# Queries' and keys' parts side by side in DRAM with fewer transfers, pairs five to seven turned from their own place, five output units held behind attention's last output

## The chip, the cores and the metric

The kernel runs as one program on one core of a Trainium2 chip. The metric is the device time of one execution in microseconds. Before the change the median of three runs is 1719.52 us (1718.66 to 1720.41).

## The reference, cut to what matters

One layer of a streaming encoder for a prompt of 1024 tokens and for 8 streams of 16 new tokens each ("samples"), width 1024, in fp32:

```python
qkv = rmsnorm(x, g_mix) @ w_in            # q, k, v of group A (8 heads of 64) and of group B (8 heads of 64)
a   = stick_breaking(q_a, k_a, v_a)       # causal, sigmoid weights, no softmax
o_b = chunk_band(q_b, k_b, v_b, rel)      # softmax over own chunk of 64 and 8 before, with a bias by distance
mix = concat(rmsnorm(a), rmsnorm(o_b))    # per head
x   = x + mix @ w_out
x   = x + (silu(h @ w_gate) * (h @ w_up)) @ w_down,   h = rmsnorm(x, g_ffn)
x   = x + sigmoid(rmsnorm(x) @ w_ple_gate) * (p @ w_ple_proj)
```

The samples attend to cached keys and values of 1024 past frames (group A) or 512 (group B). The outputs are the final norm and the new keys and values.

## The kernel before, in words

The 1024 prompt tokens are 8 row tiles of 128 and the samples one more, so there are nine. Every fp32 product is made from parts: a high part (rounded) and a low part (the rest), so that one product of two matrices is three matmuls (lines 100 to 102: high x high, low x high, high x low). The program's stages follow each other on one core: the projection of x to q, k and v; attention; the output projection; the feed-forward network; the embedding.

**Queries and keys through DRAM.** The projection leaves queries and keys transposed. `parts` cuts a group of 384 tokens into high and low, side by side in one tile `sq`; `transposed_out` (line 242) stores them to DRAM with two transfers, one into the tensor of the high parts and one into that of the low parts (`qT0h`, `qT0l`, `kT0h`, ... with 0 for group A and 1 for group B; there are 48 groups). Values are stored likewise (`v`, line 283).

**Attention** (`attention`, a generator of 137 steps) works on 8 pairs of heads, 0 to 3 of group A and 4 to 7 of group B. Each pair has 16 units: two heads by eight row tiles. When a head begins, `head` (line 531) loads its queries and keys: `qk` has 128 partitions and three parts of 1024, the queries with the high part in the first 64 partitions and the low part in the other 64, the keys' high part twice, the keys' low part twice; six transfers of 256 KB. For heads of group B `bias` then loads a table `toep` (line 553), which GpSimd negates (line 555). A unit is made in a pipeline: scores S (579, 580), weights w on ScalarE, VectorE and GpSimd, five steps later the weights' transposition (610) and its parts (614 and `sub`), two steps later for every second unit the output `po` (633, 634), which ScalarE copies to `ob` (637). After a head's last unit `turn` transposes `ob` back into `osb` (648), and after a pair's second head `finish` scales `osb` (671) and, for pairs 0 to 6, stores it to DRAM as `mixp` (674).

**What runs beside attention.** Attention's steps alternate with those of other generators: first with the rest of the projection, then with group 1 of the samples' attention over the cache (`draw`, lines 141, 405, 468; its results go out as `mixs`, line 486) and the embedding's products, and its last 36 steps with `side`. `side` is the first half of the output projection, that over pairs 0 to 3. It brings a pair's rows back from DRAM in three groups of three tiles (`mixn`, lines 894 and 898, four buffers), transposes and cuts them (904, 907, 908), loads half of the weight columns (`wraw`, then `whi` and `wlo`; two pairs of buffers), and makes 18 units, two column halves by nine tiles, each of 12 matmuls into `acc` (lines 100 to 102), one addition and one store (933, 937, 938). Then it brings pairs 4 to 6. When attention has ended, the rest of `side` is run, then pair 7, whose groups are transposed from `osb` itself but for the samples' tile, and then the weights of the second half are loaded and cut. The second half (the products `ps`), the norm and the transposition of its rows (`hrow`, line 1030) follow.

**What sets the order.** Each engine runs its instructions in one fixed order, which a framework makes from the program's order and its own planning. All transfers go through one queue, that of SyncE, and are issued in order.

Of the kernel before, what the change touches and what calls it, by code (L numbers as in the profile page):

```python
# [13 lines left out]
F32 = mybir.dt.float32  # L14
# [3 lines left out]
ALU = mybir.AluOpType  # L18
# [4 lines left out]
P = 128  # L23
D = 1024
KT = 8
NP = 8
NT = 9
HD = 64
# [4 lines left out]
SKEW = 2  # L33
R2 = 1.2
LAG, RAWS, PT = 5, 7, 2
VLAG, AHEAD = (2, 1), 2


@with_exitstack
def tile_hymba_step(  # L40
# [37 lines left out]
    nc = tc.nc  # L78
# [20 lines left out]
    def mm3(out, ah, al, bh, bl, start, stop):  # L99
        T.matmul(out, lhsT=ah, rhs=bh, start=start, stop=False)  # L100
        T.matmul(out, lhsT=ah, rhs=bl, start=False, stop=False)  # L101
        T.matmul(out, lhsT=al, rhs=bh, start=False, stop=stop)  # L102
# [111 lines left out]
    mixp = [dram.tile([P, NP, P], F32, name=f"mixp{i}") for i in range(7)]  # L214
# [12 lines left out]
    def qkv(ch, hT, stg, first, second):  # L227

        def parts(n, src, scale=1.0):
            both = stg.tile([P, 2, 384], F32R, name="sq", tag="sq")  # L230
            hl = [both[:, x, :n] for x in range(2)]
            if scale == 1.0:
                A.copy(hl[0], src)
                sub(V, hl[1], src, hl[0])
            else:
                A.activation(hl[0], src, AF.Copy, scale=scale)
                V.scalar_tensor_tensor(hl[1], src, scale, hl[0].bitcast(F32), op0=ALU.mult, op1=ALU.subtract)
            return [x.bitcast(F32) for x in hl]
# [95 lines left out]
    def decode(grp, ch, dk):  # L334
# [26 lines left out]
        parts = {}  # L361
        for what in "qk":
            for x in range(2):
                t_ = dk.tile([P, 4, P], F32, name=f"s{what}{x}", tag="slo" if x else f"s{what}", bufs=1)
                nc.sync.dma_start(t_, qkT[grp]["qk".index(what)][x][:, :, NP * P :].rearrange("c p n -> p c n"))
# [144 lines left out]
            yield  # L510


    kept = []

    def attention(ap_, ps, lag):
        def prepare(p8):
# [6 lines left out]
        def head(st, hh):  # L523

            grp, pr = st["grp"], st["pr"]
            hs = slice(hh * 64, hh * 64 + 64)
            (qh, ql), (kh, kl) = [[qkT[grp][w][x][pr] for x in range(2)] for w in range(2)]
            qk = ap_.tile([P, 3 * D], F32R, name="qk", tag="qk", bufs=2)
            for j, parts in enumerate(((qh, ql), (kh, kh), (kl, kl))):
                for i in range(2):  # L530
                    nc.sync.dma_start(qk[i * 64 : i * 64 + 64, j * D : (j + 1) * D].bitcast(F32), parts[i][hs, :D])
# [86 lines left out]
        def outputs(st, hh, g, wt):  # L618
            wth, wtl = wt
            grp = st["grp"]  # L620
            base = max(0, 2 * g - 4) if grp else 0
            nkb = 2 * g + 2 - base
            po = ps["t"].tile([P, 512], F32, name="po", tag="T")
            order = [2 * g] + [kb for kb in range(base, 2 * g + 2) if kb != 2 * g]
            for i, kb in enumerate(order):
                c0, c1 = 0, 256
                if kb == 2 * g + 1:
                    c0 = P
                if grp and kb == 2 * g - 4:
# [4 lines left out]
                T.matmul(dst, lhsT=vs, rhs=wtl[:, kb - base, c0:c1], start=False, stop=(i == nkb - 1))  # L634
# [21 lines left out]
        def finish(st):  # L656

            pr, grp, osb = st["pr"], st["grp"], st["osb"]
            ss = st["ss"].rearrange("p h t -> p (h t)")
            if grp:  # L660
                rs = st["rs"].rearrange("p h t -> p (h t)")
                V.reciprocal(rs, rs)
                V.tensor_tensor(ss, ss, rs, op=ALU.mult)
                V.tensor_tensor(ss, ss, rs, op=ALU.mult)
                r = rstd_of(ap_, ss, 2 * NP, 1.0 / HD, "o")
                G.tensor_tensor(r, r, rs, op=ALU.mult)
            else:
                r = rstd_of(ap_, ss, 2 * NP, 1.0 / HD, "o")
            for hh in range(2):
                own = osb[:, :, hh * HD : (hh + 1) * HD]  # L670
                G.tensor_tensor(own, own, r[:, hh * NP : (hh + 1) * NP].unsqueeze(2).broadcast_to([P, NP, HD]),
                                op=ALU.mult)
            if grp * 4 + pr < 7:
                nc.sync.dma_start(mixp[grp * 4 + pr], osb)

        def run(p8s):
# [42 lines left out]
    ps = {}  # L719
# [139 lines left out]
    def chain(*parts):  # L859
        for p_ in parts:  # L860
            yield from p_
# [23 lines left out]
    mp = pool(dstack, "mp", "right", 2)  # L885
    banks(dstack, "right", m=2)

    def fetch_mix(k, g):

        n = min(3, NP - g * 3)  # L890
        m = mp.tile([P, 3, P], F32, name="mixn", tag="mixn", bufs=4)
        src = m[:, :n]
        if k < 7:
            nc.sync.dma_start(src, mixp[k][:, g * 3 : g * 3 + n])
        else:
            src = pairs[7]["osb"][:, g * 3 : g * 3 + n]
        if n < 3:
            nc.sync.dma_start(m[:, 2], mixs[k // 4][:, (k % 4) * P : (k % 4 + 1) * P])
        return [src[:, o] if o < n else m[:, 2] for o in range(3)]

    def turn_mix(k, g, srcs):
        pt = ps["m"].tile([P, 384], F32, name="pt", tag="M")
        for o, src in enumerate(srcs):
            T.transpose(pt[:, o * P : (o + 1) * P], src, ident)
        h, l = hT.rows(g, k)
        gk = g_out[:, k : k + 1]
        A.activation(h, pt, AF.Copy, scale=gk)
        V.scalar_tensor_tensor(l, pt, gk, h.bitcast(F32), op0=ALU.mult, op1=ALU.subtract)

    def mix(ks):  # L910

        got = []
        for k in ks:
            while k not in done:
                yield
            for g in range(3):
                got.append((k, g, fetch_mix(k, g)))
                if len(got) > 2:
                    turn_mix(*got.pop(0))
                yield  # L920
        for x in got:
            turn_mix(*x)
            yield

    def half_out():

        yield from mix(range(4))
        for c in range(2):
            wh, wl = out_weights(0, c)
            for t in range(NT):  # L930
                cs = slice(c * 512, (c + 1) * 512)
                xs = mp.tile([P, 512], F32, name="xs", tag="xs", bufs=3)
                nc.sync.dma_start(xs, x_tok[t][:, cs])
                acc = ps["m"].tile([P, 512], F32, name="acc", tag="M")
                for k in range(4):
                    mm3(acc, *hT.tok(t, k), wh[:, k], wl[:, k], k == 0, k == 3)
                V.tensor_tensor(xs, xs, acc, op=ALU.add)
                nc.sync.dma_start(resid[t * P : (t + 1) * P, cs], xs)
                yield

    def out_weights(grp, c):

        return ch.load(w_out[0, grp * 512 : grp * 512 + 512, c * 512 : (c + 1) * 512].rearrange("(k p) c -> p k c", p=P),
                       4, 512)
# [146 lines left out]
    marks = []  # L1091

    A.activation(xg.tile([P, 1], F32, name="any", tag="r_n"), nhalf[:, 0:1], AF.Sigmoid)
    order = [0, 4, 1, 5, 2, 6, 8, 3, 7]
    xs, first_half, rows = {}, {}, []
    fetch(order[0], 0)
    with ExitStack() as planned:
# [618 lines left out]
```

## Time and profile before

| | |
|---|---|
| median of 3 runs | 1719.52 us (1718.66 to 1720.41) |
| the profiled execution | 1712.64 us |
| its span, first to last instruction | 1710.6 us |
| TensorE clock granted, mean | 0.99 |
| bytes by DMA | 293.49 MB |
| attention's last output `po` begins | 793.41 us |
| first transposition of `hrow` (L1030) | 822.69 us |

The profile shows one execution on the core. Busy time of an engine is counted without register, branch, semaphore and DMA-issuing instructions. PE is TensorE's matmul, PEld its weight load, DVE VectorE, ACT ScalarE, POOL GpSimd, SP SyncE; L904 is line 904 of the kernel. A row of the timeline has start, duration, engine, line, operation, out<-in, shape and count, and in brackets the idle time of the engine before it and what ended it. A row of a stretch has its bounds, its length, each engine's busy time with its count of instructions, the mean clock granted to TensorE, the mean busy share of the 16 DMA engines, and GB/s. In the list of DMA issues the last number is the median time from issue to landing.

### The profile page before, as it was taken

The numbers are of one execution on the slowest core, as the hardware profiler recorded it, in microseconds if no ns is written. First come the engines' busy times: TensorE is split into PE (matmuls) and PEld (weight loads), VectorE is DVE, ScalarE is ACT, GpSimd is POOL, SyncE is SP. The second block draws the span as 40 slices with busy tenths as digits, with TensorE's granted clock in tenths as the row PEclk, the third lists the DMA queues.
The fourth block names the chain that finished last, engine by engine and source line by source line (L and its number), as shares of the span: only waits on it lengthen the run. The fifth ranks groups of instructions, "written<-read, shape, count | busy, mean of one in ns | idle before, by whom it ended". The sixth has DMA issues, their size and how long they took to land.

```text
span 1710.6 us, 27738 instructions
## 1 busy us (share of the span) xinstructions
PE 1651.7 (97%) x10308; PEld 1421.3 (83%) x10308; DVE 1099.0 (64%) x1716; ACT 807.1 (47%) x1713; POOL 805.7 (47%) x652
## 2 busy tenths in 40 slices
PE   8999999989997999898989999999999999999998
PEld 7999888989996887787868888888888878878887
DVE  6111444379889666854787666666565597798875
ACT  5323545366778777643543233333332244433673
POOL 2313301277356411322345555555555379968763
PEclk9999999999998999999999999999999999999999
DMA  5847888665369885854422222222222597722222
GB/s 193 276 151 219 275 292 293 187 187 168 116 181 277 276 266 163 252 176 169 153 82 96 96 96 95 96 93 87 86 89 95 214 367 256 257 79 111 99 98 99
DMA packets 172810, 293.49 MB, mean 172 GB/s; under 512 B 16642, under 2 KB 96258, under 8 KB 170371
## 3 DMA queue, kind: packets, MB, share of 16 engines
q1 hardware_dynamic: 172674, 291.71, 52.0%
q8 instruction: 82, 1.34, 0.3%
q14 instruction: 54, 0.43, 0.1%
HBM read 204.77 MB, written 86.90 MB: 171 GB/s over the span
## 4 chain that ended last, share of the span: by engine, by line
PE 78%; DVE 7%; DMA 6%; ACT 3%; POOL 3%; issue 2%; SPq 1%; POOLq 0%; DVEq 0%; ACTq 0%
PE ps L1058 24%; PE ps L100 6%; PE ps L101 6%; PE ps L102 6%; PE pt L1321 4%; PE pt L1058 3%; PE ps L1321 3%; PE pt L610 2%; PE pt L405 2%; PE acc L468 2%; DMA v<-sv 2%; DVE keep L114 2%; PE po L634 1%; PE sdec L427 1%; PE S L579 1%
## 5 line engine op out<-in xcount | busy, mean ns | idle before, releaser
L105 POOL TENSOR_TENSOR wlo<-wraw,whi 128x512 fp32r<-128x512 f32 (+1 forms) x119 | 211.3, 1798 | 139.7 <-ACT whi L159 138.5
L100 PE MATMUL ps<-whi,hTh 128*128 128x256 f32 x576 | 167.7, 291 | 1.3 <-ACT st L267 1.3
L101 PE MATMUL ps<-wlo,hTh 128*128 128x256 f32 x576 | 164.2, 285 | 0.0
L102 PE MATMUL ps<-whi,hTl 128*128 128x256 f32 x576 | 163.7, 284 | 0.1
L159 ACT CAST whi<-wraw 128x512 fp32r<-128x512 f32 (+1 forms) x122 | 88.6, 744 | 71.4 <-PE ps L1058 28.6
L100 PEld LDWEIGHTS ps<-whi,hTh 128*128 128x128 f32 x576 | 110.4, 192 | 7.9 <-issue 5.7
L592 POOL TENSOR_TENSOR w<-w,keep 128x127 f32<-128x127 f32 (+4 forms) x64 | 78.6, 1230 | 74.8 <-DVE keep L114 64.5
L102 PEld LDWEIGHTS ps<-whi,hTl 128*128 128x128 f32 x576 | 110.4, 192 | 0.8 <-DVE hTl L105 0.4
L101 PEld LDWEIGHTS ps<-wlo,hTh 128*128 128x128 f32 x576 | 110.5, 192 | 0.2
L614 ACT CAST wth<-pt 128x512 fp32r<-128x512 f32 (+1 forms) x192 | 84.4, 466 | 44.5 <-PE pt L610 43.9
L105 DVE TENSOR_TENSOR wtl<-pt,wth 128x512 fp32r<-128x512 f32 (+1 forms) x192 | 94.1, 513 | 14.8 <-ACT wth L614 14.7
L114 DVE TENSOR_TENSOR_SCAN keep<-keep,zero 128x128 f32<-128x128 f32 (+7 forms) x64 | 101.6, 1588 | 1.7
L610 PE MATMUL pt<-ident,w 128*128 128x128 f32 x528 | 90.4, 284 | 8.5 <-DVE wtl L105 4.4
L610 PEld LDWEIGHTS pt<-ident,w 128*128 128x128 f32 x528 | 64.2, 144 | 21.6 <-DVE wtl L105 6.0
L579 PE MATMUL S<-qk 128*128 128x384 f32 (+2 forms) x192 | 71.9, 376 | 6.5 <-ACT keep L583 4.4
L633 PE MATMUL po<-wth,vk 128*128 128x256 f32 (+1 forms) x304 | 76.5, 283 | 1.5 <-DVE wtl L105 1.2
L105 POOL TENSOR_TENSOR actl<-actr,acth 128x1024 fp32r<-128x1024 f32 (+1 forms) x22 | 61.2, 2782 | 34.2 <-DMA sr<-acts 20.7
L634 PE MATMUL po<-wtl,vk 128*128 128x256 f32 (+1 forms) x304 | 73.4, 285 | 0.0
L406 DVE COPY kT<-pt 128x512 f32<-128x512 f32 x48 | 33.0, 687 | 53.4 <-PE pt L405 49.5
L101 PE MATMUL ps<-hTl,whi 128*128 128x384 f32 x192 | 65.4, 341 | 0.0
L102 PE MATMUL ps<-hTh,wlo 128*128 128x384 f32 x192 | 65.3, 340 | 0.0
L100 PE MATMUL ps<-hTh,whi 128*128 128x384 f32 x192 | 65.3, 340 | 0.0
(441 smaller groups left out, 5292.1 us busy)
## 6 DMA issues: line engine op xcount, KB each, us to landing
draw<-in_cache_sb_k SPq DMA_DIRECT2D x32, 512.0 KB, 5.7
draw<-in_cache_sb_v SPq DMA_DIRECT2D x32, 512.0 KB, 5.7
act<-sg SPq DMA_DIRECT2D x11, 1152.0 KB
actr<-act SPq DMA_DIRECT2D x22, 576.0 KB, 9.5
wraw<-in_w_in SPq DMA_DIRECT2D x11, 1024.0 KB, 8.7
wraw<-in_w_gate SPq DMA_DIRECT2D x11, 1024.0 KB, 5.5
wraw<-in_w_up SPq DMA_DIRECT2D x11, 1024.0 KB, 5.4
v<-sv SPq DMA_DIRECT2D x36, 256.0 KB, 4.7
```

The costliest lines, as they stand in the source:

```text
L100: T.matmul(out, lhsT=ah, rhs=bh, start=start, stop=False)
L101: T.matmul(out, lhsT=ah, rhs=bl, start=False, stop=False)
L102: T.matmul(out, lhsT=al, rhs=bh, start=False, stop=stop)
L105: return eng.tensor_tensor(out, a, hi.bitcast(F32), op=ALU.subtract)
L114: V.tensor_tensor_scan(rev, rev, zero[:, 0:1].to_broadcast([P, n - d]), keep[:, n - d : n - d + 1], op0=ALU.mult, op1=ALU.max)
L159: A.copy(h[:, o], v[:, o])
L579: T.matmul(sc, lhsT=hd["qq"][:, qs], rhs=hd["kkh"][:, kc], start=True, stop=False)
L610: T.transpose(pt[:, (c - c0) * P : (c - c0 + 1) * P], w[:, c * P : (c + 1) * P], ident)
L614: A.copy(wth[:, ks, qs], pv)
L634: T.matmul(dst, lhsT=vs, rhs=wtl[:, kb - base, c0:c1], start=False, stop=(i == nkb - 1))
L1058: T.matmul(out, lhsT=a[x][:, k], rhs=b[y][:, k], start=(not more and k == 0 and n == 0), stop=(k == 3 and n == 2), skip_group_check=more)
L1321: T.matmul(out, lhsT=a[i][:, x, m * P : (m + 1) * P], rhs=b[j][:, x], start=(not more and x == 0 and n == 0), stop=(x == 1 and n == 2), sk ...
```

## The change

The edit does the following:

- `qkT` is one tensor for both parts, `[4, 128, 2, 1152]`, with high and low side by side. A group is stored by one transfer instead of two (96 become 48). A head is loaded by three transfers instead of six (96 become 48): one for the queries, both parts, and two for the keys, both parts, one for each half of the partitions.
- The queries' load has a source written as `r x n -> x r n`: part, row, column, that is 2 x 64 x 1024; its destination is 128 partitions x 1024.
- `mixp` has five tensors instead of seven. Pairs 5, 6 and 7 are transposed straight from `osb` (`direct`).
- The samples' rows `mixs` are loaded whole, once, into two tiles (`own`), instead of by eight small loads. `mixn` has three buffers instead of four.
- `side` becomes `first_done(half_out())`: at each step it is asked whether pair 5, then pair 6, is done; if so that pair is turned, otherwise the next step of `half_out` is taken. `half_out` brings pairs 0 to 3, makes nine units of the first column half, four of the second, and brings pair 4.
- Five units of the second column half are held: they are made after attention's generator has ended, and are not issued before the last `po`.
- The tiles' order is `[0, 4, 1, 5, 2, 6, 8, 3, 7]` instead of 0 to 8.
- The low part of the second weight tile of the second half is made by VectorE instead of GpSimd.

```diff
-    qkT = [[[dram.tile([4, P, NT * P], F32, name=f"{nm}T{g}{n}") for n in "hl"] for nm in "qk"] for g in range(2)]
+    qkT = [[dram.tile([4, P, 2, NT * P], F32, name=f"{nm}T{g}") for nm in "qk"] for g in range(2)]
...
-        def transposed_out(grp, w, c, g, hl):
-            for x in range(2):
-                nc.sync.dma_start(qkT[grp][w][x][c, :, g * 384 : (g + 1) * 384], hl[x])
+        def transposed_out(grp, w, c, g, both):
+            nc.sync.dma_start(qkT[grp][w][c, :, :, g * 384 : (g + 1) * 384], both)
...
-            for j, parts in enumerate(((qh, ql), (kh, kh), (kl, kl))):
-                for i in range(2):
-                    nc.sync.dma_start(qk[i * 64 : i * 64 + 64, j * D : (j + 1) * D].bitcast(F32), parts[i][hs, :D])
+            nc.sync.dma_start(qk[:, :D].bitcast(F32), q.rearrange("r x n -> x r n"))
+            for i in range(2):
+                nc.sync.dma_start(qk[i * 64 : i * 64 + 64, D:].rearrange("p (x n) -> p x n", x=2).bitcast(F32),
+                                  k)
...
-            if grp * 4 + pr < 7:
+            if grp * 4 + pr < 5:
                 nc.sync.dma_start(mixp[grp * 4 + pr], osb)
...
+    own = [at.tile([P, 7 * P], F32, name="mixs0", tag="keep0")[:, :512], mp.tile([P, 512], F32, name="mixs1", bufs=1)]
+    for t_, m in zip(own, mixs):
+        nc.sync.dma_start(t_, m)
...
-        m = mp.tile([P, 3, P], F32, name="mixn", tag="mixn", bufs=4)
+        m = mp.tile([P, 3, P], F32, name="mixn", tag="mixn", bufs=3)
...
+    def direct(k):
+        for g in range(3):
+            turn_mix(k, g, sources(k, g, pairs[k]["osb"][:, g * 3 : min(g * 3 + 3, NP)]))
+            yield
...
+    def first_done(rest):
+
+        for k in (5, 6):
+            while k not in done:
+                next(rest, None)
+                yield
+            yield from direct(k)
+        yield from rest
...
-    side = chain(half_out(), mix(range(4, 7)))
+    side = first_done(half_out())
     advance(att, side, 1.0)
     for _ in side:
         pass
-    for _ in mix([7]):
+    with tc.issue_after(last_out[0].ins):
+        for t in ORDER[-HELD:]:
+            half_tile(t, 1, *held[0])
+    for _ in direct(7):
         pass
-    w_b = [out_weights(1, c) for c in range(2)]
+    w_b = [out_weights(1, c, (None, V)[c]) for c in range(2)]
```

Two places show how the instructions move. The first is SyncE's queue where attention begins: the loads of the first head, `qk`, between the last samples' rows of group A and the stores of group B's keys. Before:

```order
L486 DMA mixs_111<-ow 8x16x64 x2
L531 DMA qk<-qT0h 64x1024
L531 DMA qk<-qT0l 64x1024
L531 DMA qk<-kT0h 64x1024 x2
L531 DMA qk<-kT0l 64x1024 x2
L242 DMA kT1h<-sq 128x384
L242 DMA kT1l<-sq 128x384
```

After (`qT_70` and `kT_71` are group A's queries and keys with both parts, `kT_73` group B's keys):

```order
L488 DMA mixs_105<-ow 8x16x64 x2
L530 DMA qk<-qT_70 128x1x1024
L532 DMA qk<-kT_71 64x2x1024 x2
L243 DMA kT_73<-sq 256x1x384 x2
L543 DMA vk<-v_74 128x8x128
```

The six loads have become three, and the same holds for the other fifteen heads; each store of a group of keys or queries is one row of 256 x 384 instead of two of 128 x 384.

The second is TensorE's row behind attention's last output `po` (`pt<-ident,ob` are the transpositions of `turn`, `pt<-ident,mixn` those of a pair brought back from DRAM, `ps` the second half's products, `acc` the first half's). Before:

```order
L633 MATMUL po<-wth,vk 128x128
L634 MATMUL po<-wtl,vk 128x128
L648 MATMUL pt<-ident,ob 128x128 x4
L904 MATMUL pt<-ident,mixn 128x128
L648 MATMUL pt<-ident,ob 128x128 x2
L904 MATMUL pt<-ident,mixn 128x128 x5
L648 MATMUL pt<-ident,ob 128x128 x2
L100 MATMUL ps<-whi,hUh_9125 128x512
L101 MATMUL ps<-wlo,hUh_9125 128x512
```

After:

```order
L103 MATMUL acc<-wlo,hUh_9038 128x512
L104 MATMUL acc<-whi,hUl_9039 128x512
L636 MATMUL po<-wtl,vk 128x128
L650 MATMUL pt<-ident,ob 128x128 x6
L102 MATMUL acc<-whi,hUh_9040 128x512
L103 MATMUL acc<-wlo,hUh_9040 128x512
L104 MATMUL acc<-whi,hUl_9041 128x512
```

Units of the first half now stand right before the last `po` and between and behind the transpositions of the last `ob`, where before pairs brought back from DRAM and the second half's products stood.

More of the change, by code (lines that the diff above doesn't have):

```diff
@@ L35 @@
 LAG, RAWS, PT = 5, 7, 2
+HELD = 5
+ORDER = [0, 4, 1, 5, 2, 6, 8, 3, 7]
 VLAG, AHEAD = (2, 1), 2
@@ L923, in mix, with half_tile @@
             yield
+    def direct(k):
+        for g in range(3):
+            turn_mix(k, g, sources(k, g, pairs[k]["osb"][:, g * 3 : min(g * 3 + 3, NP)]))
+            yield
+    def half_tile(t, c, wh, wl):
+        cs = slice(c * 512, (c + 1) * 512)
+        xs = mp.tile([P, 512], F32, name="xs", tag="xs", bufs=3)
+        nc.sync.dma_start(xs, x_tok[t][:, cs])
+        acc = ps["m"].tile([P, 512], F32, name="acc", tag="M")
+        for k in range(4):
+            mm3(acc, *hT.tok(t, k), wh[:, k], wl[:, k], k == 0, k == 3)
+        V.tensor_tensor(xs, xs, acc, op=ALU.add)
+        nc.sync.dma_start(resid[t * P : (t + 1) * P, cs], xs)
     def half_out():
@@ L929, in half_out, with out_weights @@
             wh, wl = out_weights(0, c)
[L930 to L938, printed above, removed]
-                yield
-    def out_weights(grp, c):
-        return ch.load(w_out[0, grp * 512 : grp * 512 + 512, c * 512 : (c + 1) * 512].rearrange("(k p) c -> p k c", p=P),
-                       4, 512)
-    side = chain(half_out(), mix(range(4, 7)))
+            if c:
+                held.append((wh, wl))
+            for t in ORDER if c == 0 else ORDER[:-HELD]:
+                half_tile(t, c, wh, wl)
+                yield
+        yield from mix([4])
+    def first_done(rest):
[5 more added lines that the diff above has]
+        yield from rest
+    def out_weights(grp, c, eng=None):
+        src = w_out[0, grp * 512 : grp * 512 + 512, c * 512 : (c + 1) * 512].rearrange("(k p) c -> p k c", p=P)
+        return ch.parts(ch.raw(src, 4, 512), 4, 512, 2, eng)
+    held = []
+    side = first_done(half_out())
     advance(att, side, 1.0)
```

30 lines of the change are left out of this document (12 added, 18 removed).

## Prediction

> **What bounds the kernel now.** I read the page first, then the busy time by stretches, then the waits and the chain. The page says which engine has no room:
>
> ```profile
> PE 1651.7 (97%) x10308; PEld 1421.3 (83%) x10308; DVE 1099.0 (64%) x1716; ACT 807.1 (47%) x1713; POOL 805.7 (47%) x652
> ```
>
> TensorE works 97% of the span, so a gain is TensorE's idle or slow time, and a loss is any new wait of TensorE. The stretches where the first half of the output projection runs (us, then busy time of PE, PEld, DVE, ACT, POOL, then clock, DMA share, GB/s):
>
> ```profile
> 690.00:700.00 10.00, 9.23 (x66) 8.70 (x64) 9.67 (x31) 9.11 (x26) 5.55 (x7) 0.84 0.89 271
> 700.00:710.00 10.00, 6.82 (x56) 6.47 (x55) 5.03 (x17) 6.17 (x16) 1.53 (x1) 1.00 1.04 288
> 710.00:720.00 10.00, 9.96 (x60) 8.83 (x59) 10.00 (x30) 8.92 (x26) 0.58 (x3) 0.83 0.89 226
> 720.00:790.00 70.00, 70.00 (x396) 60.34 (x395) 36.63 (x95) 26.12 (x64) 12.07 (x9) 1.00 0.50 169
> 790.00:800.00 10.00, 9.22 (x63) 7.66 (x62) 5.35 (x11) 6.70 (x12) 5.91 (x3) 1.00 0.74 245
> 800.00:810.00 10.00, 6.10 (x26) 4.48 (x25) 2.47 (x4) 2.18 (x4) 4.01 (x4) 0.83 0.57 201
> 810.00:820.00 10.00, 9.71 (x50) 7.78 (x49) 5.50 (x11) 4.68 (x11) 0.55 (x1) 1.00 0.27 102
> ```
>
> Between 720 and 790 TensorE has no gap. The gaps lie at the start (700 to 710) and behind the last output of attention (800 to 810). TensorE's rows in order of time, with its wait in brackets, name them:
>
> ```profile
> 688.61 0.55 PE L904 MATMUL pt<-ident,mixn 128*128 128x128 f32 x3 [2.18 <-DMA mixn<-mixp]
> 708.85 0.55 PE L904 MATMUL pt<-ident,mixn 128*128 128x128 f32 x3 [3.18 <-DMA mixn<-mixp]
> ...
> 793.41 0.28 PE L634 MATMUL po<-wtl,vk 128*128 128x128 f32 x1
> ...
> 806.11 1.51 PE L904 MATMUL pt<-ident,mixn 128*128 128x128 f32 x6 [3.87 <-DMA mixn<-mixp]
> ```
>
> The last `po` is at 793.41; the long wait behind it, 3.87 us, is for a pair's rows that come back from DRAM. The second thing to see is how full the 16 DMA engines are while attention runs, since the change rewrites what they carry:
>
> ```profile
> 324.00:344.00 20.00, 19.36 (x158) 18.83 (x157) 6.25 (x12) 5.96 (x17) 4.75 (x10) 1.00 0.98 250
> 344.00:420.00 76.00, 71.02 (x540) 67.59 (x539) 63.65 (x77) 54.32 (x139) 55.75 (x59) 1.00 0.56 169
> 520.00:640.00 120.00, 111.58 (x978) 91.12 (x977) 92.33 (x230) 89.34 (x233) 52.35 (x61) 0.93 0.90 272
> 640.00:670.00 30.00, 28.69 (x255) 22.21 (x253) 18.75 (x65) 20.00 (x56) 6.50 (x11) 1.00 0.52 146
> 670.00:730.00 60.00, 52.90 (x347) 47.60 (x345) 43.77 (x129) 41.40 (x109) 16.72 (x16) 0.94 0.83 232
> 730.00:790.00 60.00, 60.00 (x340) 51.58 (x339) 31.54 (x81) 23.50 (x56) 9.96 (x6) 1.00 0.47 163
> ```
>
> From 520 to 640, where decode group 1 streams its cache, the DMA engines are 90% busy: little is left for any of them.
>
> **The change, part by part.**
>
> *Held units and pairs turned from their own place.* Behind the last `po` now stand five units of twelve matmuls, and pairs 5 to 7 need no rows from DRAM. The price of a unit's matmul is the distance of two starts:
>
> ```profile
> 720.10 0.39 PE L101 MATMUL acc<-wlo,hUh 128*128 128x512 f32 x1
> 720.32 0.39 PE L102 MATMUL acc<-whi,hUl 128*128 128x512 f32 x1
> ...
> 802.13 1.04 POOL L671 TENSOR_TENSOR osb<-osb,r_o 128x512 f32<-128x512 f32 x1
> ...
> 811.70 0.55 PE L904 MATMUL pt<-ident,osb 128*128 128x128 f32 x3 [0.29 <-DVE hUl L908]
> ```
>
> Sixty matmuls at about 0.22 us are 13 us. Pair 7's `osb` is finished by two such operations of 1.04 us from 802.13 on, so at 804.2, 10.8 us behind the last `po`: the held units cover it. What goes is the idle time from 790 to 820, 0.78 + 3.90 + 0.29 = 5.0 us, and the clock of 0.83 in 800 to 810, at most 1.7 us: together 6.7 us. What comes: the second half's weights can be converted only when the held units have read the slot. I charge 1 us, since pair 7's nine groups stand between. So -5.7 us. The bounds: if the waits of 2.18 and 3.18 us go too (no rows of pairs 5 and 6, no small loads of sample rows), -11; if three `mixn` buffers instead of four bring as many waits at the start as go at the end, +1.
>
> *Weight subtraction from GpSimd to VectorE, sample rows loaded once, mixp with five stores.* VectorE is busy 5.50 of 10 us where its subtraction would come, and these stores and loads end no wait but the ones named: 0.
>
> *Fewer transfers.* Bytes stay; SyncE issues 96 transfers fewer. TensorE could only gain where issues hold it up; from 324 to 344 it is idle 0.64 us, so -0.5.
>
> *The form of the queries' load.* Before, each half of a head's queries is a load of 64 rows of 4 KB. Now one load brings both, and its source is written with the part (high, low) as the outermost of three steps: 2 x 64 x 1024, where the destination has 128 rows. Every large load of before has 64 rows or more outermost.
>
> ```profile
> draw<-in_cache_cb_k SPq DMA_DIRECT2D x16, 512.0 KB, 4.7
> mixs<-ow SPq DMA_DIRECT2D x16, 32.0 KB
> ...
> L531 SPq DMA_DIRECT2D qk<-qT0h x8: 450/450/521, 324.1 to 496.3; - x8
> ...
> L531 SPq DMA_DIRECT2D qk<-qT1h x8: 450/475/501, 522.1 to 713.5; - x8
> ```
>
> If the load spreads over all 16 engines, as the 512 KB cache load that lands in 4.7 us, the cost is 0. If it is divided by its outermost step, two engines carry 262,144 bytes each. The only repeated transfer of before with a small outermost step, `mixs<-ow` with 8, is too small (32 KB) to show a time, and no view prints over how many engines it went. I take the narrow end as the likelier, because a division by the first step is the plain one and the forms so far never had to show another. The Trainium skill ("DMA: Bandwidth & Descriptors", section on why a DMA increments its semaphore by 16) states this as a rule: the number of engines is the largest up to 16 that divides the slowest dimension of both sides, here 2. By it the narrow price below holds; by the wide reading this term is 0 and the sum is the first rival's. No view of before shows two engines at work.
>
> The narrow price, at the pace of the fullest stage: 272 GB/s / 16 / 0.90 = 18.9 GB/s an engine, so 13.9 us on two engines, against 1.7 us when all share it: 12.2 us more for each of the 16 heads. From 522.1 to 713.5 there are eight. From 520 to 730 an engine has 0.90 x 120 + 0.52 x 30 + 0.83 x 60 = 173 us of work; with 8 x 12.2 = 98 it is 271 in 210 us. Every other transfer has its share on those two engines, so all come late by up to 61 us. The cover: a cache load is issued well ahead of its reader.
>
> ```profile
> 591.40 0.53 SPq L141 DMA_DIRECT2D draw<-in_cache_cb_k  x1
> ...
> 608.15 1.04 PE L405 MATMUL pt<-ident,draw 128*128 128x128 f32 x8
> ```
>
> 608.15 - 591.40 - 4.7 = 12 us. That leaves 49. At 324 two heads' loads come within 8 us, one at 324.1 and the next here:
>
> ```profile
> 332.41 0.45 SPq L531 DMA_DIRECT2D qk<-qT0h  x1
> ```
>
> That is 0.98 x 20 + 24 = 44 us of work in 20, 24 behind; half of that I count, as the chain runs there through such transfers and the values' stores already hold ScalarE:
>
> ```profile
> 327.95 6.41 DMA kT1h<-sq
> 336.35 8.56 DMA v<-sv
> ...
> 649.58 7.24 DMA toep<-in_rel_table
> 683.71 4.86 DMA mixn<-mixp
> 701.74 7.07 DMA mixn<-mixp
> ```
>
> ```profile
> POOL toep L555 <- DMA toep<-in_rel_table: 41.8, 5, 13.0
> ACT sv L280 <- DMA v<-sv: 18.6, 8, 5.0
> ```
>
> So the upper end is 49 + 12 = 61 us. For the lower end the engines keep a faster pace when only two are at work, that of 730 to 790: 163 / 16 / 0.47 = 21.7 GB/s, 12.1 us a load, 10.6 more than shared. The work from 520 to 730 shrinks to (272 x 120 + 146 x 30 + 232 x 60) / 347 = 147 us (16 x 21.7 = 347 GB/s together); 147 + 85 = 232 in 210, 22 behind, 10 after the cover, and nothing at 324. Between 10 and 61 I take the middle, 35: neither row is nearer, since the stage is full at 272 GB/s and half empty behind it. The rows above name where it would bite: the bias table, loaded right behind a head's queries and awaited by GpSimd five times, and `mixn`, for which TensorE already waits.
>
> **The sum.** The profiled execution took 1712.64 us (span 1710.6), 6.9 under the median of 1719.52. -5.7 - 0.5 + 35 = +28.8 gives 1741.4 as a profile, 1748.3 beside the median. The case's own range: with 10 and 61 us, and +1 in place of -5.7 above, 1723 to 1781.
>
> **The rivals.**
> *First, faster: the queries' load costs nothing,* because it spreads over 16 engines or because every late transfer still lands before its reader. For it speaks that TensorE waits for a DMA only once from 520 to 690, the 2.18 us quoted, and that a cover of 12 us is as long as one load's price. Against it: 271, or at best 232, us of work in 210. Then only -6.2 is left: 1713.3. It decides as long as the lag stays under 12 us. Chance 0.17.
> *Second, no change: the load spreads, but the gain is not there.* With all of attention's early side work moved forward, VectorE and ScalarE set the pace from 690 to 720 (DVE 9.67 and 10.00 of 10 us in two rows), and what the tail gives back is paid here: 5.7 us, so 1719.0. Against it stand 33 us of spare VectorE time from 720 to 790. Chance 0.05.
> *Third, the narrow load bites at the start and little behind.* Late transfers from 324 on cost 12 us, decode's cover holds and no more than 0 to 5 comes on top: 1719.5 - 6.2 + 12 = 1725, at least 1719 if half of the 12 is hidden. Chance 0.10, of which 0.03 is no change.
>
> **How the numbers follow.** The forecast, narrow load with 10 to 61 us, has 0.68. A measurement of this kernel can tell about 0.2%, 3.4 us. Faster is the first rival alone, 0.17; within 0.2%, the second and 0.03 of the third, 0.08; slower, 0.68 + 0.07 = 0.75. The range takes in the first rival's 1713 with its bound (1711) and the upper end, 1782; outside lie a gain of over 8 us (0.06) and delays that add up beyond 61 us, since the front was counted by half (0.08).
>
> **What would show it.** Right: transfers of 4 KB rows whose landing after a queries' load takes 10 us and more; new TensorE waits on `draw`, `mixn`, or on ScalarE behind `v<-sv`; GpSimd's wait for the bias table over 41.8 us in total; a DMA share that falls in 520 to 640 while the stage grows. The tail right: no wait on `mixn` behind the last `po`, and `acc` matmuls there. Wrong: decode's stage as long as before and `qk` landing in 4 to 6 us; then the load is wide, and the time is near 1713. If the tail shows a wait for `osb` or for the weights instead, the first term is wrong.

## The result, and the profile after

The changed kernel takes 1857.89 us (median of 6 runs, 1853.47 to 1859.91), the kernel before 1718.08 us in the same runs: ratio 1.0818, 95% interval 1.0804 to 1.0831. That is 140 us slower, where the prediction had 1748 and a range of 1711 to 1782. The direction was right and so was the transfer that was named; its price, 35 us, was nearly four times too low (129 us by q_wide below).

The profiled execution spans 1856.0 us. Engines, from the page of the changed kernel:

```profile
PE 1682.8 (91%) x10308; PEld 1445.9 (78%) x10308; DVE 1096.3 (59%) x1718; ACT 806.6 (43%) x1713; POOL 798.9 (43%) x650
```

The number of matmuls is the one of before, yet TensorE is now busy 91% of the span: 173 us of idle time against 59. Of the 145 us by which the span grew 114 are idle time; in the other 31 TensorE is busy for longer with the same matmuls, at a mean granted clock of 0.956 against 0.990. The stretches of the changed kernel where attention runs (start to end, length, then busy time of PE, PEld, DVE, ACT, POOL, clock, DMA share, GB/s):

```profile
333.00:353.00 20.00, 9.14 (x77) 8.94 (x75) 1.45 (x3) 1.58 (x4) 0.00 (x0) 0.83 0.58 140
353.00:450.00 97.00, 71.62 (x514) 69.41 (x515) 51.86 (x71) 45.96 (x119) 42.93 (x59) 0.82 0.48 127
450.00:553.00 103.00, 93.97 (x616) 88.97 (x614) 81.77 (x112) 65.37 (x157) 52.94 (x64) 0.98 0.46 133
553.00:711.00 158.00, 123.03 (x911) 99.53 (x913) 97.32 (x212) 93.29 (x236) 57.11 (x72) 0.86 0.71 204
711.00:790.00 79.00, 58.37 (x503) 47.84 (x496) 37.32 (x126) 38.90 (x110) 12.40 (x18) 0.85 0.53 140
790.00:845.00 55.00, 36.03 (x230) 31.31 (x229) 28.90 (x89) 29.50 (x76) 14.05 (x12) 0.81 0.68 168
```

TensorE idles in every one of them, and the clock column falls to 0.81 to 0.86 where it idles most. The sign that matters is the last pair of columns. One might look for full DMA engines in a kernel that waits for transfers. Here the mean share fell: from 553 to 711 it is 0.71 with 204 GB/s, where the corresponding stretch of before (520 to 640) had 0.90 and 272. A mean over sixteen engines does not tell whether a few of them hold the rest up.

The trace does tell it, by the updates of semaphores, the counters by which a transfer reports its landing. In the kernel before, 752 transfers have 16 updates, the 16 small `mixs<-ow` with an outermost step of 8 have nine, and one load with a single row has two; where there are fewer than 16, the first comes 0.4 to 1.1 us after the issue, ahead of the others. Read so, there is one update for each DMA engine that takes part, and one at the issue where not all do. In the changed kernel all 16 queries' loads have three: one at the issue and two at the end. These are some transfers of its trace around one such load:

| issued at, us | transfer | updates | us from issue to the updates |
|---|---|---|---|
| 627.95 | `qk<-qT` | 3 | 0.9; 18.5 and 19.4 |
| 628.53 | `qk<-kT` | 16 | fourteen from 5.1 to 5.8; 19.5 and 20.2 |
| 637.41 | `draw<-in_cache_cb_v` | 16 | fourteen from 3.6 to 4.1; 13.5 and 15.0 |
| 640.73 | `toep<-in_rel_table` | 16 | fourteen from 4.3 to 5.1; 12.4 and 13.9 |
| 663.11 | `draw<-in_cache_cb_k` | 16 | sixteen from 3.2 to 3.5 |

So fourteen shares of a transfer land within 6 us here and two land late, behind the queries. In 97 transfers of the changed kernel the last two updates come over 3 us behind the fourteenth, in all 32 loads of keys among them; in the kernel before there is none. The queries themselves land 15.4 to 27.9 us after their issue.

The chain that ended last, in the order of time, shows what this holds up (start, length, transfer; other pieces left out):

```profile
627.95 19.36 DMA qk<-qT
647.38 11.23 DMA wraw<-in_w_out
684.25 15.40 DMA proj<-pjo
711.58 20.32 DMA toep<-in_rel_table
750.72 20.19 DMA toep<-in_rel_table
790.54 20.14 DMA qk<-kT
826.35 17.31 DMA mixn<-mixp
844.71 16.76 DMA mixn<-mixp
```

Between 627 and 862 there are 141 us of transfers on the chain, and only one is the queries' load itself. The others are weights, a store (`proj<-pjo`), bias tables, keys and rows of a pair. Before, the bias table at 649.58 had 7.24 us there, and `mixn` 4.86 and 7.07. Two waits that the prediction quoted have grown:

```profile
POOL toep L557 <- DMA toep<-in_rel_table: 87.4, 5, 21.6
ACT sv L281 <- DMA v<-sv: 37.2, 6, 14.8
```

They were 41.8 and 18.6 us. When the first head's queries are asked for, the changed kernel is 8.4 us late (332.58 against 324.13). By TensorE's rows it is 21 us late at the first scores `S`, 54 when group A is nearly through, and 125 at the last `po`, with part of the first half's work still to come:

```profile
918.84 0.22 PE L636 MATMUL po<-wtl,vk 128*128 128x128 f32 x1
```

In the kernel before this row is at 793.41.

### The profile page after: what moved, and what is told of

Its sections match the earlier page's. It is cut to its first block, busy times and chain, and to the rows that moved or that the text cites. A ratio compares the mean times of both kernels' runs of the same rounds, so it can differ in the third digit from the quotient of the medians.

```text
span 1856.0 us, 27556 instructions
## 1 busy us (share of the span) xinstructions
PE 1682.8 (91%) x10308; PEld 1445.9 (78%) x10308; DVE 1096.3 (59%) x1718; ACT 806.6 (43%) x1713; POOL 798.9 (43%) x650
## 4 chain that ended last, share of the span: by engine, by line
PE 48%; DMA 9%; DVE 3%; ACT 2%; POOL 2%; issue 2%; SPq 0%; POOLq 0%; DVEq 0%; ACTq 0%
PE ps L1083 23%; PE pt L1346 4%; PE ps L1346 3%; PE pt L1083 3%; DMA toep<-in_rel_table 2%; DMA mixn<-mixp 2%; PE ps L102 1%; PE ps L104 1%; PE ps L103 1%; DMA qk<-kT 1%; PE pt L612 1%; DMA qk<-qT 1%; PE pt L104 1%; PE pt L103 1%; PE pt L102 1%
## 5 line engine op out<-in xcount | busy, mean ns | idle before, releaser
L107 POOL TENSOR_TENSOR wlo<-wraw,whi 128x512 fp32r<-128x512 f32 (+1 forms) x117 | 205.3, 1779 | 141.1 <-ACT whi L161 139.8
L581 PE MATMUL S<-qk 128*128 128x384 f32 (+2 forms) x192 | 76.8, 401 | 58.9 <-DMA qk<-kT 23.0
L581 PEld LDWEIGHTS S<-qk 128*128 128x128 f32 x192 | 39.6, 206 | 69.1 <-issue 27.1
L612 PEld LDWEIGHTS pt<-ident,w 128*128 128x128 f32 x528 | 65.8, 149 | 34.6 <-POOL w L594 12.4
L635 PE MATMUL po<-wth,vk 128*128 128x256 f32 (+1 forms) x304 | 81.0, 296 | 2.5 <-DVE wtl L107 2.4
L407 PE MATMUL pt<-ident,draw 128*128 128x128 f32 x384 | 55.3, 286 | 21.9 <-ACT kT L408 10.1
L107 POOL TENSOR_TENSOR sv<-st,sv 128x256 fp32r<-128x256 f32 x36 | 31.1, 867 | 93.3 <-ACT sv L281 92.4
```

What stands on the lines that cost most here:

```text
L107: return eng.tensor_tensor(out, a, hi.bitcast(F32), op=ALU.subtract)
L581: T.matmul(sc, lhsT=hd["qq"][:, qs], rhs=hd["kkh"][:, kc], start=True, stop=False)
L612: T.transpose(pt[:, (c - c0) * P : (c - c0 + 1) * P], w[:, c * P : (c + 1) * P], ident)
```

## The experiments

Each ratio is to the kernel before, run on the same chip, with its 95% interval. Differences in us are taken from the ratios, at 1717 us.

**The queries by two loads of 64 rows, the rest as changed** (q_wide).

```diff
-            nc.sync.dma_start(qk[:, :D].bitcast(F32), q.rearrange("r x n -> x r n"))
+            for x in range(2):
+                nc.sync.dma_start(qk[x * 64 : x * 64 + 64, :D].bitcast(F32), q[:, x])
```

> The changed kernel, but a head's queries are loaded by two transfers of 64 rows each (one for the high part, one for the low), from the same tensor with both parts side by side. Theory N (narrow load): nearly all of the 140 us came from the one transfer whose outermost step is 2, so the time falls from 1857.9 to between 1712 and 1740. Rival R (all transfers with three steps are slow, the groups' stores and the keys' loads as well): it stays above 1800, since 48 stores and 32 loads of keys keep their form. Rival T (the tail): the 18 us that TensorE lost between the last po and the first hrow stay as they are, so not below 1735.

Measured: 1727.67 us, ratio 1.0067 (1.0054 to 1.0079). So 129 of the 140 us hang on the form of this one load, 16 times in the program. The stores and the keys' loads, which also have three steps, keep their form here, so rival R is out: with the rest of the change they are left with 12 us. The tail is not where the loss is either. In this kernel's trace every queries' load has 16 updates, and no transfer has two of them late.

**The narrow load alone, in the kernel before** (narrow_only).

```diff
-            for j, parts in enumerate(((qh, ql), (kh, kh), (kl, kl))):
+            nc.sync.dma_start(qk[:, :D].bitcast(F32), qboth[grp][pr, hs, :, :D].rearrange("r x n -> x r n"))
+            for j, parts in enumerate(((kh, kh), (kl, kl))):
```

> The kernel before with one edit: the queries' high and low parts lie side by side in DRAM and a head's queries are loaded by the one transfer of the change; stores stay two a group, the keys' loads four a head, and the output projection's order is that of before. Theory N: 1718 plus 90 to 140 us, so 1808 to 1858. Rival R: within 10 us of 1718.

Measured: 1821.74 us, ratio 1.0611 (1.0596 to 1.0626): 105 us. With the number of stores, the keys and the output projection as they were, the load is enough. All its 16 queries' loads have three updates, and 119 transfers have their last two late. The chain of this kernel, between 646 and 815, has the same look as that of the whole change:

```profile
646.63 17.76 DMA mixp<-osb
664.45 8.61 DMA proj<-pjo
686.00 17.89 DMA toep<-in_rel_table
724.11 17.09 DMA toep<-in_rel_table
760.56 16.72 DMA qk<-kT1h
777.30 6.80 DMA mixn<-mixp
797.03 17.25 DMA mixn<-mixp
```

**The other transfers of the change, with the queries by two loads, in the kernel before** (merge_wide): `qkT` with both parts side by side, one store a group, two loads of keys a head.

```diff
-                nc.sync.dma_start(qkT[grp][w][x][c, :, g * 384 : (g + 1) * 384], hl[x])
+            nc.sync.dma_start(qkT[grp][w][c, :, :, g * 384 : (g + 1) * 384], both)
...
+            for x in range(2):
+                nc.sync.dma_start(qk[x * 64 : x * 64 + 64, :D].bitcast(F32), q[:, x])
```

> The kernel before with all of the transfers' part of the change (one store a group, two loads for the keys), but the queries loaded by two transfers of 64 rows. Theory N with the early loss seen in the changed kernel's trace, where TensorE is 8.4 us late before the first head is loaded: 1720 to 1728. If that early loss belongs to the narrow load or to the rest of the change: 1716 to 1719. Rival R: above 1800.

Measured: 1733.58 us, ratio 1.0098 (1.0080 to 1.0115): 17 us slower, more than the 2 to 10 us that theory N gave. Fewer transfers made the kernel slower.

**A group stored by two transfers again, the rest as in merge_wide** (two_stores).

```diff
-            nc.sync.dma_start(qkT[grp][w][c, :, :, g * 384 : (g + 1) * 384], both)
+            for x in range(2):
+                nc.sync.dma_start(qkT[grp][w][c, :, x, g * 384 : (g + 1) * 384], both[:, x])
```

> The kernel before with both parts side by side in DRAM, the keys loaded by two transfers a head and the queries by two, but a group stored by two transfers as before. Theory O (the 17 us of the merged transfers come from the stores: a group is stored when both parts are there, and near 80 us a weight load went ahead of it in the queue): the 8 us near 80 us go, 1716 to 1724. Rival K (the keys' loads of 512 KB cost it): stays at 1730 to 1735.

Measured: 1722.71 us, ratio 1.0036 (1.0023 to 1.0049): 11 us come back. The place is near 80 us. In the changed kernel, the last store of group A's keys and a weight load on SyncE's queue, and ScalarE's next row, which needs the stored tile's buffer:

```profile
85.22 0.38 SPq L143 DMA_DIRECT2D wraw<-in_w_in  x1
85.70 1.21 SPq L243 DMA_DIRECT2D kT<-sq  x2
...
92.91 0.49 ACT L238 ACTIVATE sq<-ps 128x384 fp32r<-128x384 f32 x1 [9.68 <-DMA kT<-sq]
...
94.04 0.69 PE L102 MATMUL ps<-hTh,whi 128*128 128x384 f32 x1 [6.54 <-DVE sq L239]
```

The same place in the kernel before, and in two_stores:

```profile
82.01 0.88 SPq L242 DMA_DIRECT2D kT0l<-sq  x2
82.99 0.41 SPq L141 DMA_DIRECT2D wraw<-in_w_in  x1
...
84.15 0.49 ACT L236 ACTIVATE sq<-ps 128x384 fp32r<-128x384 f32 x1 [2.68 <-DMA kT0l<-sq]
```

```profile
81.18 1.78 SPq L242 DMA_DIRECT2D kT<-sq  x4
83.05 0.41 SPq L141 DMA_DIRECT2D wraw<-in_w_in  x1
```

The order of stores and weight load has turned round. A store of both parts can start only when VectorE has the low part; the order that came out puts 1 MB of weights ahead of it, and ScalarE waits 9.68 us in place of 2.68; in merge_wide the same order stands there, and this wait is 9.50 us. That the merged stores cause the loss is shown; that it is the weight load ahead of them, and not the form of the store, is read from the rows and was not tried by itself.

**The held units and the rest alone, with queries' and keys' transfers as before** (held_only).

```diff
-    qkT = [[dram.tile([4, P, 2, NT * P], F32, name=f"{nm}T{g}") for nm in "qk"] for g in range(2)]
+    qkT = [[[dram.tile([4, P, NT * P], F32, name=f"{nm}T{g}{n}") for n in "hl"] for nm in "qk"] for g in range(2)]
...
-            nc.sync.dma_start(qkT[grp][w][c, :, :, g * 384 : (g + 1) * 384], both)
+            for x in range(2):
+                nc.sync.dma_start(qkT[grp][w][x][c, :, g * 384 : (g + 1) * 384], hl[x])
```

> The changed kernel with the transfers of queries and keys as before (separate tensors, two stores a group, six loads a head): only the held units, the pairs turned from their own place, the samples' rows loaded once and the order of tiles are left of the change. The prediction's first term: 5.7 us less than before, so about 1712. Rival T (the tail of the changed kernel's trace is its own cost): 1718 plus 10 to 18, so 1728 to 1736.

Measured: 1714.04 us, ratio 0.9981 (0.9967 to 0.9994): 3.3 us faster, between 1 and 5.7. TensorE's waits behind the last `po` of this kernel, and the first `hrow`:

```profile
789.24 0.55 PE L907 MATMUL pt<-ident,mixn 128*128 128x128 f32 x3 [1.81 <-DVE xs L938]
813.02 0.50 PE L102 MATMUL ps<-whi,hUh 128*128 128x512 f32 x1 [2.79 <-ACT hUh L910]
825.64 1.03 PE L1055 MATMUL pt<-ident,hrow 128*128 128x128 f32 x8
```

The wait of 3.87 us for `mixn` is gone. In its place stand 1.81 us for VectorE's addition of a held unit and 2.79 us for ScalarE's cut of a pair, 4.6 us in all. These rows tell the waits, not the gain: the profiled execution of this kernel took 1716.11 us, more than the 1712.64 of the one before, so the 3.3 us rest on the medians alone.

**Queries and keys interleaved row by part, three loads a head, the rest as changed** (interleaved). The source of the queries' load is then 128 rows at one distance.

```diff
-            nc.sync.dma_start(qk[:, :D].bitcast(F32), q.rearrange("r x n -> x r n"))
+            nc.sync.dma_start(qk[:, :D].bitcast(F32), q.rearrange("r x n -> (r x) n"))
             for i in range(2):
-                nc.sync.dma_start(qk[i * 64 : i * 64 + 64, D:].rearrange("p (x n) -> p x n", x=2).bitcast(F32),
-                                  k)
+                nc.sync.dma_start(qk[i::2, D:].rearrange("p (x n) -> p x n", x=2).bitcast(F32), k)
```

> The changed kernel with as few transfers as it has, but the partitions of qk ordered row by part instead of part by row: the queries' source is then 128 rows at one distance and its outermost step counts 128; the keys go to every second partition. Theory N (the narrow form, not the number or size of transfers, costs the 130 us): as with two loads, 1727.7 plus or minus 4. Rival S (one transfer of 512 KB is slower than two of 256 KB because it is awaited whole): above 1745.

Measured: 1712.94 us, ratio 0.9979 (0.9969 to 0.9988). The same bytes, the same number of transfers, the same 512 KB in one: 144 us less than the change. Size and number are cleared, the order of the steps is what costs; each queries' load has 16 updates again. It is also 15 us better than the two loads of q_wide, more than theory N had.

**The narrow load in group A's heads alone, in the kernel before** (narrow_A; as narrow_only, but `if grp == 0`, else two loads of 64 rows).

> The kernel before with the narrow queries' load for the eight heads of group A alone; group B's heads load them by two transfers of 64 rows. With all sixteen narrow it was 105 us slower, and in that trace 38 of 111 us were lost by the end of group A. Theory N, each load delays what is queued behind it: 1716 plus 30 to 40, so 1746 to 1756. The prediction's sum had 0 to 12 here: 1716 to 1728.

Measured: 1761.12 us, ratio 1.0260 (1.0243 to 1.0276): 45 us for eight heads, more than the 30 to 40 expected and far from 0 to 12, mostly in a stretch whose DMA share was 0.56 (344 to 420). That leaves 60 of the 105 for group B's eight; a kernel with the load in group B alone was not run.

**The narrow load on ScalarE's queue, in the kernel before** (narrow_act).

```diff
-            nc.sync.dma_start(qk[:, :D].bitcast(F32), qboth[grp][pr, hs, :, :D].rearrange("r x n -> x r n"))
+            nc.scalar.dma_start(qk[:, :D].bitcast(F32), qboth[grp][pr, hs, :, :D].rearrange("r x n -> x r n"))
```

> The kernel before with the narrow queries' load in all heads, issued on ScalarE's queue instead of SyncE's. Theory L (the load fills two of the sixteen engines, and every other transfer waits for its share on these two behind it, whatever queue it came by): 1800 to 1840, since 13 us on two engines stay. Rival Q (the loss comes of the order in SyncE's queue: transfers behind the load, and issues that are held up): 1720 to 1760.

Measured: 1810.51 us, ratio 1.0553 (1.0537 to 1.0569): 95 us remain. Where the load is issued matters by 10 us, and 83 transfers still have their last two updates late; rival Q is out as the main cause.

**The narrow load behind the head's keys and bias table** (narrow_last; narrow_only with that line moved to the end of `head`).

> The kernel before with the narrow queries' load in all heads, but issued after the head's keys and its bias table instead of ahead of them. Theory D (the loss falls on what is queued directly behind the load: keys, table): clearly less than the 105 us of the load ahead of them, 1740 to 1780. Theory U (the two engines have more work than time, the prediction's reckoning, so it does not matter which transfer comes first): 1800 to 1825.

Measured: 1801.20 us, ratio 1.0501 (1.0485 to 1.0518): 86 us. That is one fifth less, far from theory D's 1740 to 1780 and at the lower end of theory U's range. The lateness does not go to the keys and the table alone: whatever is issued in the next 15 us or so comes late, and here the queries themselves come later too.

**Half of the columns narrow** (narrow_half).

```diff
+            nc.sync.dma_start(qk[:, :512].bitcast(F32), qboth[grp][pr, hs, :, :512].rearrange("r x n -> x r n"))
+            for x in range(2):
+                nc.sync.dma_start(qk[x * 64 : x * 64 + 64, 512:D].bitcast(F32), qboth[grp][pr, hs, x, 512:D])
```

> The kernel before, the first 512 columns of a head's queries by a narrow load and the other 512 by two loads of 64 rows: half the bytes on two engines. If each microsecond that two engines are behind costs alike: half of 105, so 1760 to 1775. If there is a cover of 12 us that a load of 7 us stays within, as the prediction had it: 1716 to 1730.

Measured: 1761.60 us, ratio 1.0261 (1.0242 to 1.0281): 45 us, for half the bytes 43% of the loss. A cover of 12 us everywhere would have hidden it.

The loss does not come evenly. Below is how late TensorE is against the kernel before, in us, each time at the same matmul of `S`, named by its start in the kernel before. From about 540 on group B's loads act.

| start before, us | narrow_A | narrow_only | narrow_half |
|---|---|---|---|
| 332.4 | 10 | 8 | 8 |
| 360.3 | 20 | 19 | 14 |
| 389.4 | 30 | 28 | 17 |
| 445.5 | 38 | 36 | 19 |
| 519.8 | 41 | 39 | 17 |
| 539.5 | 43 | 42 | 23 |
| 555.9 | 43 | 53 | 23 |
| 619.1 | 44 | 66 | 23 |
| 666.0 | 43 | 86 | 36 |
| 694.5 | 43 | 96 | 42 |
| 759.9 | 46 | 108 | 49 |

In group A the first three loads cost nearly 30 us and the next five 13 or 14; in group B each costs mostly 6 to 11. Half a load costs next to nothing from 389 to 520 and from 556 to 619. So there is cover in some stretches and none in others.

**All together, with two stores a group** (best; interleaved with the edit of two_stores).

> The interleaved kernel with a group of queries or keys stored by two transfers, as before the change; the loads, the held units and the rest stay as there. Theory O (the merged stores cost about 10 us near 80 us of the span, by the queue's order): 1712.9 minus 8 to 11, so 1702 to 1705. Rival W (later waits of attention take it up): 1710 to 1715.

Measured: 1707.19 us, ratio 0.9948 (0.9935 to 0.9961): the fastest of the study, 5.3 us below interleaved by the ratios, less than the 8 to 11 expected. Its engines, from the page:

```profile
PE 1647.3 (97%) x10308; PEld 1418.8 (83%) x10308; DVE 1094.9 (64%) x1718; ACT 808.1 (47%) x1713; POOL 796.7 (47%) x650
```

**The interleaved loads and two stores without the held units** (inter_before; the kernel before with only these).

> The kernel before with both parts side by side, two stores a group as before, and the interleaved loads (one for the queries, two for the keys a head); the output projection's order is that of before. If the parts add up: the kernel of the two stores and four loads was at 1.0036 of before, the interleaved loads were worth 14.7 us where the rest of the change stood beside them, so about 1708. Rival H (the loads' gain needs the held units): 1716 to 1722.

Measured: 1710.76 us, ratio 0.9970 (0.9954 to 0.9986). Against two_stores (1.0036) the only difference is one queries' load in place of two and the order of partitions: 11 us, without the held units' help. Against best, the held units are worth 3.8 us more, about their 3.3 alone.

**The held units with the narrow load, and all merged transfers without the held units** (held_narrow, merge_only). Two kernels for the 24 us by which the narrow load costs more in the changed kernel (129) than in the kernel before (105).

> The kernel with the held units alone (transfers as before), plus the narrow queries' load: without the narrow load it was at 0.9981 of before. If the narrow load costs the 105 us that it costs in the kernel before: 1714 plus 105, so 1815 to 1824. If it costs more because the held units leave less work beside attention: 1830 to 1845.

> The kernel before with all of the transfers' part of the change, the narrow queries' load included; the output projection's order is that of before. With the queries loaded by two transfers it was at 1.0098 of before. If the parts add up: 1733 plus 105, so 1833 to 1843. If the narrow load costs more where the keys come by two transfers of 512 KB instead of four: 1850 to 1860, like the whole change.

Measured: 1828.14 us, ratio 1.0646 (1.0624 to 1.0668), and 1851.82 us, ratio 1.0784 (1.0761 to 1.0808). Against their partners without the narrow load (0.9981 and 1.0098) it costs 114 and 118 us here. So both parts deepen it, by 9 and 13 us, each uncertain by about 5, and 105 + 9 + 13 = 127 is nearly the 129 of the whole change.

## Why the prediction was wrong, point by point

**What bounds the kernel.** That TensorE has no slack, so that any new wait is time, held. In every experiment with the narrow load its idle time is most of what grew; in the changed kernel 31 of 145 us are longer busy time, for which the prediction had no term.

**The queries' load.** The form was the right one to name, and so was the price of one load. Two DMA engines were reckoned at 12.1 to 13.9 us without the way there and back; in the changed kernel the loads land after 15.4 us at least, on two late updates each, where a load of group A's high parts before landed after 4.0 in the median. The rule of the Trainium skill ("DMA: Bandwidth & Descriptors", section on why a DMA increments its semaphore by 16), two engines for an outermost step of 2, agrees with this trace: three updates for a queries' load, of which one comes at the issue and two at the end, and 16 for the interleaved load. The trace of before held the same sign in the nine updates of `mixs<-ow`, though no view prints it.

**The step that failed: from late transfers to late work.** For group A the prediction had 0 to 12 us, all of it at the first two heads. For the other six heads it had no term and gave no reason; its own row has a DMA share of 0.56 there. Measured: 45 us. By the table, 20 are lost with the first two heads and nearly as much again by 445. A transfer issued behind the load comes late even where the engines are half free, and something that already waits stands behind it: in narrow_A up to 575 us ScalarE waits 32.6 us for the values' stores `v<-sv`, against 11.1 in the kernel before up to 520, and TensorE 9.2 us for keys.

For group B the prediction added up 271 us of work on two engines in 210, so a backlog that grows to 61 us; it took off 12 us of cover, read from one cache load, which left 49. With group A's 12 that is 61 again, and the 35 us are the middle between this and a lower end of 10. Measured, by difference, the eight heads cost 60 us in the kernel before, and 66 by the table from 540 on. That is near the backlog of 61 without cover, but the nearness is in part luck. A backlog that grew through the stage would leave two updates late all the time. In narrow_only, before seven of group B's eight queries' loads, the last transfers land with all sixteen updates within 2 us, so the two engines had caught up. What adds up is a wait of TensorE for each head, 6 to 11 us for most. One cache load with 12 us to spare was taken for all transfers; the waits for `toep` and `v<-sv`, quoted right beside it, already had none. So the term of 35 us should have been 105 alone, 42 to 45 in group A and 60 to 66 in group B.

**What multiplied it.** In the changed kernel the load costs 129 us, by 9 more with the held units and by 13 more with the merged transfers. The prediction added its terms as if each stood alone; measured alone they are 105, 17 and -3 us, 119 together, where the change costs 140. Which transfers carry the extra was not tried.

**Held units and pairs turned from their own place.** Predicted 5.7 us faster with bounds of -11 and +1; measured 3.3. The wait for `mixn` went as said, and no wait for `osb` came. The 1 us charged for what is late next was too little: 1.81 and 2.79 us of new waits, for the held units' additions and for the last pair's cut.

**Fewer transfers.** Predicted 0.5 us faster; measured 17 us slower with the queries' load wide. Of these 11 are the merged stores, by an order in the queue that the prediction did not look for: it counted the stores and did not compare their place with the weight load's. The rest, 6 us (two_stores, 1.0036), was not taken apart; the order of the partitions and one queries' load in place of two turn it into a gain.

**The rivals.** The first (the load costs nothing) is out by 129 us, the second (the load spreads, but no gain) by the same and by held_only's gain. The third, a bite at the start and little behind, named a place that does lose (20 us with the first two heads), but the loss went on behind it in both groups. The range ended at 1782, because its upper end was 49 us for group B, with the cover taken off, and 12 for half of the front; it left nothing for group A's other heads, for merged stores or for what the parts do to each other.

## What to carry to other kernels

When transfers are merged, look at the outermost step of both sides, not at their number: a small outermost count took the place of 64 and 128 rows here, and 16 loads of 512 KB cost 105 to 129 us, while the same bytes with the order of the partitions changed made the kernel faster than before. A late transfer is not priced by the mean share of the DMA engines, by a sum of work over a stage or by one reader with time to spare; go head by head, and look for the readers that already wait right behind the load. Here the same load cost from about 2 to 11 us by what stood behind it, and half of it cost nothing in some stretches. A store that is merged waits for its last part, and in one queue it can fall behind a large load; compare the order there before counting what was saved.

## What the runs showed of the hardware that was not expected

The mean share of the sixteen DMA engines fell when two of them became the limit: 0.71 at 204 GB/s in the changed kernel's stretch from 553 to 711, against 0.90 at 272. The transfers that use all sixteen land with the two slowest shares, 7 us and more behind the other fourteen in the table above. And SyncE's issues themselves became long. Its rows of the queries' load in the changed kernel (duration in ns, least, median, most):

```profile
L530 SPq DMA_DIRECT2D qk<-qT x16: 522/540/8322, 332.6 to 836.7; - x16
L532 SPq DMA_DIRECT2D qk<-kT x32: 518/593/4017, 333.2 to 846.3; - x32
```

Before, the longest issue of a queries' high part was 0.52 us, and no issue on SyncE took more than 3.1. In the changed kernel eleven take more than 5, a store of values 13.2 us the longest, and such an issue holds the whole queue behind it. That the load costs 10 us less from ScalarE's queue may be this (SyncE's longest issue is 7.2 us in narrow_act and 9.3 in narrow_only); it was not separated from the mere place in the queue.
